# A mixer-and-experts layer on one core: expert biases split on 128 partitions, the largest expert moved within the order of experts

## The chip, the cores and the metric

The kernel runs on one NeuronCore of a Trainium2 chip. The metric is device time in microseconds (us) of one execution; lower is better. TensorE is called PE below, VectorE DVE, ScalarE ACT, GpSimd POOL and SyncE SP.

## The reference

One layer over 512 tokens of width 1024: four head groups run side by side (stick-breaking attention, a gated linear recurrence, HGRN2, Mamba-2) from one input projection, then an output projection with a residual, then a mixture of 32 experts, of which each token takes 4, and a last RMSNorm. Cut to the part that the change touches:

```python
logits = (xt @ router_w + router_b).astype(jnp.float32)
top_logits, top_idx = lax.top_k(logits, TOP_K)
gates = jax.nn.softmax(top_logits, axis=-1)
def run_block(args):              # rows of one expert e
    tok, e = args
    hmid = xt[tok] @ w_gu[e] + b_gu[e]
    glu = jnp.minimum(hmid[:, 0::2], SWIGLU_LIMIT)
    lin = jnp.clip(hmid[:, 1::2], -SWIGLU_LIMIT, SWIGLU_LIMIT)
    act = glu * jax.nn.sigmoid(SWIGLU_ALPHA * glu) * (lin + 1.0)
    return act @ w_down[e] + b_down[e]
```

The weights of one expert are w_gu (1024 x 2048) and w_down (1024 x 1024) in float32: 12 MiB. All 32 experts are read, 384 MiB.

## The kernel before

**The mixer part** (tile_kernel) comes first. Its order is written out by hand: strings such as ORD1 and ORD2, in which each letter calls one step of one generator. In ORD1 the letters d are steps of the Mamba-2 loop (d_loop: VectorE multiplies decay blocks by score blocks at L1874, PE uses them at L1880, the output is scaled at L1885 and L1886), s are steps of the HGRN2 state (c_state), b is the normalisation of the recurrence (L1465 to L1472), and the seven letters m are the steps of moe_biases. After ORD1 come the products with w_out (L1823), whose weights ACT and DVE split in two (L1817, L1818), interleaved by ORD2 with the last normalisations; then ORD3, in which the router runs and the weights of the experts start to stream in.

**moe_biases** (L120 to L151) turns the two bias tables of 32 x 2048 and 32 x 1024 into parts that a matrix product can add up exactly: each bias of w_gu into three bfloat16 parts that lie on partitions 0-31, 32-63 and 64-95 of the tile bgu, each bias of w_down into a float32r part, the same again, and the rest, in the tile bd. It loads each half of a table three times, one copy per group of 32 partitions (L130), and then rounds (ACT) and subtracts (DVE) in place, on 96 or on 32 partitions by 1024 columns. Its ACT steps are L138, L141, L142, L145 (twice each) and L149, its DVE steps L139, L143 (twice each) and L150.

**The experts** (moe) run in the order of the string SEQ. H stands for a large expert (up to 128 rows, more than 64), L for one with 64 rows, B for one with 32. The number of rows is a fixed capacity by the rank of the expert's count (CAPS); the H of the string with number BIG, counted from 0, is the largest expert: 128 rows as an H unit and 32 more as a B unit beside it. So before, the largest expert is the third H, expert number 7 of the order (counted from 0).

- An H unit uses three float32r products per weight block: the rows and the weights are both split into a high and a low part. ACT (L613) and DVE (L614) split each block of 128 x 1024 weights just before PE uses it (three(), L629), with three split buffers (NSP).
- An L or B unit feeds float32 weights straight to PE (L658 for w_gu, L729 and L724 for w_down).
- For expert j of the order, PE does the bias product (L644) and w_gu of j (gemm1), then the activation is started (act), then PE does w_down of expert j-1 (gemm2). When j-1 is an H, the outputs of the units before it are added to the rows of the tokens by products with one-hot matrices S (add, L789 on PE and L791 on DVE), interleaved with gemm2; with the largest expert they all stand before gemm2.
- yout scales and splits the output of a unit (ACT L742 and L761, DVE L744 and L763). For the largest expert it does the B unit first, whose output lies on 32 partitions at a time, four ACT and four DVE instructions.
- The rows of an expert are fetched by an indirect DMA on POOL (fetch, L568) and turned by PE (turn, L585). turn_at calls the turns of the groups that a table (where) puts at that place. That table follows from SEQ: the rows of an H form a group of their own, those of L and B units are put together, up to 128. Before, the group of experts 8 and 10 is turned right after the largest expert's gemm1 (place M at j = 7). prepare() makes one-hot matrices and fetches rows ahead.

**The weights** are read by SP in pieces of 1 MiB, 8 for w_gu and 4 for w_down, in the order in which PE uses them (Loads). They go round 11 places (pools ring and more; two further places at the beginning). A piece is read once the piece 11 before it has been used: by the split of an H, by the products of an L. SP takes its queue strictly in order; in front of the weights it has the loads of x into acc (L1958).

**The first expert** (j = 0) runs its gemm1 beside the rest of the router's tables, a generator called first, of nine steps: one step after each of the eight w_gu pieces, and, by the argument of mid, one more in the middle of pieces 4 to 7.

**The end**: gemm2 of the last expert is interleaved with add of the expert before it; hot builds the one-hot matrices S (L770) for both just ahead.

Of the kernel before, what the change touches and what calls it, by code (L numbers as in the profile page):

```python
# [21 lines left out]
F32 = mybir.dt.float32  # L22
FR = mybir.dt.float32r
BF = mybir.dt.bfloat16
I32 = mybir.dt.int32
U32 = mybir.dt.uint32
AF = mybir.ActivationFunctionType
OP = mybir.AluOpType
# [23 lines left out]

CAPS = (160, 120, 104, 104, 96, 96, 88, 80, 80, 72, 72, 72, 72) + 16 * (64,) + (32, 64, 64)

SEQ, BIG = "LL" + 4 * "HLHLL" + 3 * "HL" + "HBHL", 2
NSP = 3
FIN = "aaqqrAQrASQrAQrSSss"

# [59 lines left out]

def moe_biases(tc, a, bp, st, r_):

    nc = tc.nc
    bgu = bp.tile([96, 2048], BF, name="bgu")
    bd = bp.tile([96, D], FR, tag="yS", name="bd")
    r_["b"] = bgu, bd
    bst = [st[0:96, 0:1024], st[0:96, 1024:2048]]

    def load(f):
        src = a["moe_b_down"][0] if f == 2 else a["moe_b_gu"][0, :, 1024 * f:1024 * f + 1024]
        for s in range(3):
            nc.gpsimd.dma_start(bst[f % 2][32 * s:32 * s + 32, :], src)  # L130

    load(0)
    load(1)
    yield
    for f in range(2):
        cols = slice(1024 * f, 1024 * f + 1024)
        b = bst[f]
        nc.scalar.activation(bgu[:, cols], b, AF.Copy)  # L138
        nc.vector.tensor_tensor(b, b, bgu[:, cols], op=OP.subtract)  # L139
        yield  # L140
        nc.scalar.activation(bgu[32:64, cols], b[32:64, :], AF.Copy)  # L141
        nc.scalar.activation(bgu[64:96, cols], b[64:96, :], AF.Copy)  # L142
        nc.vector.tensor_tensor(b[64:96, :], b[64:96, :], bgu[64:96, cols], op=OP.subtract)  # L143
        yield
        nc.scalar.activation(bgu[64:96, cols], b[64:96, :], AF.Copy)  # L145
        if f == 0:
            load(2)
    yield
    nc.scalar.activation(bd, bst[0], AF.Copy)  # L149
    nc.vector.tensor_tensor(bd[64:96, :], bst[0][64:96, :], bd[64:96, :].bitcast(F32), op=OP.subtract)  # L150
    yield  # L151


# [325 lines left out]
def moe(ctx, tc, a, out, acc, c, loads, rt, mp, mp_es, hp, s2p, bp, early, once_es):  # L479

    nc = tc.nc
# [4 lines left out]
    def bank():  # L486
        return ps["m"].tile([128, 512], F32, name="m")

    def pair():

        return hp.tile([128, 1024], F32, name="h")
# [19 lines left out]
    cols = {x: [r for r, n in enumerate(CAPS) if n in ns] for x, ns in (("H", range(65, 129)), ("L", (64,)), ("B", (32,)))}  # L511
# [8 lines left out]
    N = len(seq)  # L520
# [125 lines left out]
    def gemm1(us, chunk, k, splits, limit, mid=lambda: None):  # L646

        W = chunk(k)
        last = k == KD - 1
        for u in us:  # L650
            if u.kind == "H":
                for half in range(2):
                    wh, wl = splits.take()
                    three(u.h[2 * half:2 * half + 2], u.xH[:, k, :], u.xL[:, k, :], wh, wl, False, last)
                    splits.make(limit)
            else:
                for q in range(4):
                    nc.tensor.matmul(u.h[q], u.xT[:, k, :], W[:, 512 * q:512 * q + 512], start=False, stop=last)  # L658
                    if q == 1:
                        mid()  # L660
# [104 lines left out]
    def hot(us):  # L765

        for u in us:
            if u.S is None:
                u.S = wk.tile([128, T], FR, name="S", bufs=3)[0:u.m]
                nc.vector.tensor_scalar(u.S, iota[0:u.m, :], u.tok[0:u.m, :], None, op0=OP.is_equal)  # L770
# [22 lines left out]
    splits = Splits([loads.of(j) for j, us in enumerate(seq) if us[0].kind == "H"])  # L793
# [3 lines left out]
    for g, us in enumerate(groups):  # L797
        j = us[0][0].j
# [21 lines left out]
    def turn_at(x, j, banks):  # L820
        for g in where.get((x, j), []):
            while g not in have:
                prepare()
            turn(g, *have[g], banks())
            turned.add(g)

    two = lambda: [bank(), bank()]
    halves2 = lambda: (lambda h: [h[:, 0:512], h[:, 512:1024]])(pair())

    def steps(*gens):  # L830
        for g in gens:
            yield from g

    def run(g, n=1000):
        for _ in range(n):
            if next(g, "end") == "end":
                return
# [5 lines left out]
    first = steps(rt.tables(), rt.more())  # L843
# [6 lines left out]
            ids(seq[e][0])  # L850
            yield

    pending = []
    for j, us in enumerate(seq):
        u = us[0]
        kind = u.kind
        if j == 1:
            once_es.close()
            sp = splits.pool = ctx.enter_context(tc.tile_pool(name="sp", bufs=NSP))
        if j == 2:  # L860
            mp_es.close()
            hL = ctx.enter_context(tc.tile_pool(name="hL", bufs=1, space=PSUM, side="right"))
            ps["m"] = ctx.enter_context(tc.tile_pool(name="m2", bufs=2, space=PSUM, side="right"))
        if j >= 1:
            loads.before(j + 1)

        if j == 0:
            u.views, u.h = [(0, rt.h0[0])], rt.h0[1]
        else:
            hL_ = [pair() if j < 2 else hL.tile([128, 1024], F32, name="hL")] if us[-1].kind != "H" else None  # L870
            light = lambda: hL_
            for x in us:
                if x.kind == "H":
                    x.bk = [pair(), pair()]
                bias(x, x.bk if x.kind == "H" else light() if x.kind == "L" else [light()[0][:, 0:512]])
        hi = heavy.index(j) if kind == "H" else 0
        after = heavy.index(j - 1) if j and seq[j - 1][0].kind == "H" else None
        for k in range(KD):
            if j == 0:
                gemm1(us, loads.of(j), k, splits, (hi, 16), lambda: run(first, k > 3))  # L880
                run(first, 1)
                continue
            gemm1(us, loads.of(j), k, splits, (hi, 16))
            if j == 1:
                if k == 0:
                    run(first)
                elif k < 5:
                    prepare()
                if k == 3:
                    back(seq[0])  # L890
                if k == 5:
                    mine = own()
                if k > 4:
                    run(mine, 2 if k == 7 else 1)
            elif k % 2:
                prepare()
            if kind == "H" and k == 2:
                turn_at("A", j, two)
            if kind != "H" and j > 1:
                if k == 3:  # L900
                    hot(pending)
                if after is not None and k > 4:
                    splits.make((after, 24), 1)
        act(us)
        if j == 0:
            continue
        if j > 1:
            turn_at("M", j, halves2 if kind != "H" and j > 1 else (lambda: [hL_[0][:, 512:1024], bank()]) if len(us) > 1 else two)

        prev = seq[j - 1]  # L910
        pk = prev[0].kind
        if pk == "H":
            hot(pending)
            limit = (after, 24) if kind != "H" and not (j + 1 < N and seq[j + 1][0].kind == "H") else (after + 1, 16)
            if len(prev) > 1:
                for i in range(NT):
                    add(pending, i)
        else:
            limit = None
        if j == 1:  # L920
            bd = rt.bdown()
        for f in range(KD):
            if pk == "H" and len(prev) == 1 and pending and 0 < f <= NT:
                add(pending, f - 1)
            gemm2(prev, loads.of(j - 1), f, splits, limit, u.views[0][1][:, 512:1024] if len(prev) > 1 else None)
            if j == 1:
                run(bd, 1)
                if f == 2:
                    turn_at("M", j, two)
                if f == 5:  # L930
                    back(us)
            elif pk != "H" and f in (2, 5):
                prepare()
            if pk == "H" and f == 4 and kind != "H":
                back(us)
            if f == 6 and len(us) > 1:
                back(us[1:])
            if pk == "H" and f == 5:
                turn_at("B", j, halves2)
            if pk != "H" and j + 1 < N and seq[j + 1][0].kind == "H" and f > 4:  # L940
                splits.make((heavy.index(j + 1), 16), 1)
        if pk == "H":
            pending = []
        pending = pending + prev
        yout(prev)
        if j > 1 and (pk != "H" or kind == "H"):
            back(us[:1])

# [62 lines left out]
    with tc.If(nblk > 0):  # L1011
        with tc.For_i(0, nblk, 1) as b, tc.manual_schedule():
# [11 lines left out]
            def chunk(q):  # L1024
                if q not in got:
                    got[q] = moe_chunk(nc, loads.slots, a, reg, q)
                return got[q]
# [999 lines left out]
```

## Time and profile before

| | us |
|---|---|
| median of 3 runs | 1378.11 |
| lowest and highest run | 1372.44, 1380.81 |
| the profiled execution, its own time | 1376.71 |
| its span, first to last instruction | 1374.9 |
| PE busy in the span | 1312.0 (95%) |
| DVE busy | 882.4 (64%) |
| ACT busy | 643.6 (47%) |
| read from HBM | 436.68 MB |

The profiled execution lies 1.4 us below the median, and 1.8 us of it are outside the span. The mixer part fills the span up to about 330 us, the experts follow, the last norm takes the end from about 1355 us. In rows of the trace an instruction is given as line, engine, operation, out<-in, shapes and count; what stands in square brackets is the idle time of that engine just before it and what ended it.

### The profile page before, as it was taken

The numbers are of one execution on the slowest core, as the hardware profiler recorded it, in microseconds if no ns is written. First come the engines' busy times: TensorE is split into PE (matmuls) and PEld (weight loads), VectorE is DVE, ScalarE is ACT, GpSimd is POOL, SyncE is SP. The second block draws the span as 40 slices with busy tenths as digits, with TensorE's granted clock in tenths as the row PEclk, the third lists the DMA queues.
The fourth block names the chain that finished last, engine by engine and source line by source line (L and its number), as shares of the span: only waits on it lengthen the run. The fifth ranks groups of instructions, "written<-read, shape, count | busy, mean of one in ns | idle before, by whom it ended". The sixth has DMA issues, their size and how long they took to land.

```text
span 1374.9 us, 17788 instructions
## 1 busy us (share of the span) xinstructions
PE 1312.0 (95%) x6460; PEld 768.3 (56%) x6460; DVE 882.4 (64%) x1215; ACT 643.6 (47%) x886; POOL 94.4 (7%) x162
## 2 busy tenths in 40 slices
PE   7999998898999999999999999999999999999994
PEld 6877773574365554456545655546544555464651
DVE  5457867675576754457546765748545667686865
ACT  5366667652154533336234542526334445454632
POOL 0000123020110002000010000200010000000001
PEclk9999997899999999999999999999999999999998
DMA  6312012087899999888999999999999999999982
GB/s 196 116 61 92 1 70 88 1 325 306 338 398 405 420 419 397 339 363 310 404 366 419 419 394 420 409 419 405 419 400 419 419 393 420 418 417 399 419 359 78
DMA packets 80801, 442.09 MB, mean 322 GB/s; under 512 B 10972, under 2 KB 25380, under 8 KB 31684
## 3 DMA queue, kind: packets, MB, share of 16 engines
q1 hardware_dynamic: 76708, 427.66, 77.7%
q0 software_dynamic: 3856, 12.72, 2.7%
q8 instruction: 52, 0.85, 0.3%
q10 hardware_dynamic: 144, 0.52, 0.1%
q14 instruction: 41, 0.34, 0.1%
HBM read 436.68 MB, written 4.19 MB: 321 GB/s over the span
## 4 chain that ended last, share of the span: by engine, by line
PE 77%; DMA 7%; DVE 7%; ACT 5%; issue 3%; POOL 1%; DVEq 0%; SPq 0%; ACTq 0%; POOLq 0%
PE h L629 18%; PE hL L658 14%; PE m L629 10%; PE m L729 7%; PE m L1198 6%; PE h L789 6%; DMA wch<-in_moe_w_down_dram 4%; DMA wch<-in_moe_w_gu_dram 3%; PE h L658 2%; DVE w L614 1%; PE h L1823 1%; PE m L1823 1%; PE h L696 1%; PE m L1202 1%; PE h L585 1%
## 5 line engine op out<-in xcount | busy, mean ns | idle before, releaser
L614 DVE TENSOR_TENSOR w<-wch,w 128x1024 fp32r<-128x1024 f32 x312 | 378.8, 1224 | 153.8 <-ACT w L613 145.5
L613 ACT ACTIVATE w<-wch 128x1024 fp32r<-128x1024 f32 x312 | 328.4, 1061 | 273.4 <-DMA wch<-in_moe_w_down_dram 98.7
L629 PE MATMUL h<-w,xx 128*72 128x512 f32 (+6 forms) x1248 | 301.9, 399 | 4.9 <-DVE w L614 4.5
L629 PEld LDWEIGHTS h<-w,xx 128*72 128x72 f32 (+6 forms) x1248 | 195.6, 159 | 102.8 <-DVE w L614 7.2
L658 PE MATMUL hL<-wch,xp 128*64 128x512 f32 (+1 forms) x1152 | 239.1, 593 | 1.1 <-DMA wch<-in_moe_w_gu_dram 1.1
L658 PEld LDWEIGHTS hL<-wch,xp 128*64 128x64 f32 (+1 forms) x1152 | 74.8, 134 | 148.8 <-issue 141.2
L729 PE MATMUL m<-wch,aTL 128*64 128x512 f32 x544 | 124.3, 603 | 0.2 <-DVE tg L557 0.2
L629 PE MATMUL m<-w,aH 128*72 128x512 f32 (+6 forms) x416 | 116.5, 400 | 3.4 <-ACT w L613 2.1
L675 ACT ACTIVATE ag<-ag 128x512 f32<-128x512 f32 (+7 forms) x46 | 28.6, 622 | 167.9 <-DVE ag L674 167.8
L629 PEld LDWEIGHTS m<-w,aH 128*72 128x72 f32 (+6 forms) x416 | 62.9, 158 | 39.7 <-issue 7.4
L565 POOL CAST ix<-tg 64x1 int32<-64x1 f32 (+8 forms) x31 | 19.0, 611 | 848.3 <-DVE tg L557 839.7
L791 DVE TENSOR_TENSOR acc<-acc,h 128x1024 f32<-128x1024 f32 (+1 forms) x61 | 72.9, 1198 | 6.4 <-PE h L789 6.4
L729 PEld LDWEIGHTS m<-wch,aTL 128*64 128x64 f32 x544 | 37.0, 138 | 69.2 <-issue 67.2
L763 DVE SCALAR_TENSOR_TENSOR yS<-m,tg,yS 64x512 fp32r<-64x512 f32 (+1 forms) x38 | 28.5, 750 | 71.4 <-ACT yS L761 71.0
L1198 PE MATMUL m<-uH,wh 128*128 128x512 f32 x176 | 71.9, 408 | 0.8 <-DVE uL L1305 0.8
L1198 PE MATMUL m<-uH,wl 128*128 128x512 f32 x176 | 70.1, 398 | 0.5 <-DVE wl L1164 0.4
L1198 PE MATMUL m<-uL,wh 128*128 128x512 f32 x176 | 69.9, 397 | 0.0
L629 PE MATMUL m<-w,aL 128*72 128x512 f32 (+6 forms) x208 | 65.1, 394 | 0.0
L761 ACT ACTIVATE yS<-m,tg 64x512 fp32r<-64x512 f32 (+1 forms) x38 | 25.9, 681 | 74.9 <-PE m L729 72.4
L789 PE MATMUL h<-yS,S 128*128 128x512 f32 (+1 forms) x168 | 54.9, 400 | 2.4 <-DVE acc L791 1.3
L674 DVE TENSOR_SCALAR ag<-hL 128x512 f32<-128x512 f32 (+1 forms) x18 | 11.9, 659 | 64.5 <-PE hL L658 64.5
L1164 DVE TENSOR_TENSOR wl<-wnat,wh 128x1024 fp32r<-128x1024 f32 (+1 forms) x26 | 31.5, 1223 | 30.3 <-ACT wh L1163 30.3
(500 smaller groups left out, 1634.0 us busy)
## 6 DMA issues: line engine op xcount, KB each, us to landing
wch<-in_moe_w_gu_dram SPq DMA_DIRECT2D x256, 1024.0 KB
wch<-in_moe_w_down_dram SPq DMA_DIRECT2D x127, 1024.0 KB
wnat<-in_w_in_dram SPq DMA_DIRECT2D x12, 1024.0 KB
wch<-in_w_out_dram SPq DMA_DIRECT2D x4, 1024.0 KB
xin<-in_x_dram SPq DMA_DIRECT2D x4, 512.0 KB
acc<-in_x_dram SPq DMA_DIRECT2D x4, 512.0 KB
xdr<-wch POOLq DMA_DIRECT2D x4, 512.0 KB, 7.5
out_dram<-fo SPq DMA_DIRECT2D x3, 512.0 KB
```

The costliest lines, as they stand in the source:

```text
L613: nc.scalar.activation(wh, w, AF.Copy)
L614: nc.vector.tensor_tensor(wl, w, wh.bitcast(F32), op=OP.subtract)
L629: nc.tensor.matmul(ps_[q], x, w[:, 512 * q:512 * q + 512], start=start and z == 0, stop=stop and z == 2)
L658: nc.tensor.matmul(u.h[q], u.xT[:, k, :], W[:, 512 * q:512 * q + 512], start=False, stop=last)
L675: nc.scalar.activation(g, g, AF.Gelu_apprx_sigmoid)
L729: nc.tensor.matmul(u.y[0][64 * dh:64 * dh + 64, :], u.aT[:, 2 * (f // 4) + f % 2, (f // 2) % 2, :], W[:, 512 * dh:512 * dh + 512], start=f ...
L763: nc.vector.scalar_tensor_tensor(u.yS[o_, dh, :], y[s_, :], u.gate[s_, :], u.yS[s_, dh, :].bitcast(F32), op0=OP.mult, op1=OP.subtract)
L789: nc.tensor.matmul(hh[:, 512 * dh:512 * dh + 512], s, y, start=z == 0, stop=z == len(todo) - 1)
L791: nc.vector.tensor_tensor(o, o, hh[:, cols], op=OP.add)
L1164: nc.vector.tensor_tensor(wl, w, wh.bitcast(F32), op=OP.subtract)
L1198: nc.tensor.matmul(s.p, s.ws[q // 2][:, k, :], u_[:, k, :], start=(k == 0 and q == 0), stop=(k == KD - 1 and q == 2))
L1823: nc.tensor.matmul(p, m_(x, k)[:, 128 * i:128 * i + 128], ww, start=(k == 0 and q == 0), stop=(k == KD - 1 and q == 2))
```

## The change

The bias tables are loaded once, on 128 partitions: a quarter of the columns on each group of 32 partitions, so that a step on 128 partitions has 512 (or 256) columns. The parts are made in a scratch tile and moved to their place in bgu and bd by 24 copies, 12 issued by SP and 12 by POOL. In the order of experts the second pair of L experts moves from places 20 and 21 to 26 and 27, and the largest expert becomes the fifth H, number 12 of the order. The extra B unit's output is evicted after two pieces of the next expert's gemm1 (late) and not ahead of them; turn_at for place M of the largest expert moves into gemm2 of the expert before; the first expert's extra router steps come in pieces 6 and 7 only; S for the last two units is built in the loop.

By the table where, the new order puts the 32 extra rows of the largest expert (12) into one group with the rows of expert 13, and this group and that of the largest expert's 128 rows are both turned at place M of j = 11. No group falls on place M of j = 12.

```diff
-SEQ, BIG = "LL" + 4 * "HLHLL" + 3 * "HL" + "HBHL", 2
+SEQ, BIG = "LL" + 3 * "HLHLL" + 4 * "HL" + "HLLHBHL", 4
...
-    bst = [st[0:96, 0:1024], st[0:96, 1024:2048]]
-
-    def load(f):
-        src = a["moe_b_down"][0] if f == 2 else a["moe_b_gu"][0, :, 1024 * f:1024 * f + 1024]
-        for s in range(3):
-            nc.gpsimd.dma_start(bst[f % 2][32 * s:32 * s + 32, :], src)
-
-    load(0)
-    load(1)
+    g, d = st[:, 0:512], st[:, 512:768]
+    parts = st[:, 768:1536].bitcast(BF).rearrange("p (s f) -> p s f", s=3)
+    dH, dL = st[:, 1536:1792].bitcast(FR), st[:, 1792:2048].bitcast(FR)
+    for q in range(4):
+        nc.gpsimd.dma_start(g[32 * q:32 * q + 32, :], a["moe_b_gu"][0, :, 512 * q:512 * q + 512])
+        nc.gpsimd.dma_start(d[32 * q:32 * q + 32, :], a["moe_b_down"][0, :, 256 * q:256 * q + 256])
     yield
-    for f in range(2):
-        cols = slice(1024 * f, 1024 * f + 1024)
-        b = bst[f]
-        nc.scalar.activation(bgu[:, cols], b, AF.Copy)
-        nc.vector.tensor_tensor(b, b, bgu[:, cols], op=OP.subtract)
-        yield
-        nc.scalar.activation(bgu[32:64, cols], b[32:64, :], AF.Copy)
-        nc.scalar.activation(bgu[64:96, cols], b[64:96, :], AF.Copy)
-        nc.vector.tensor_tensor(b[64:96, :], b[64:96, :], bgu[64:96, cols], op=OP.subtract)
-        yield
-        nc.scalar.activation(bgu[64:96, cols], b[64:96, :], AF.Copy)
-        if f == 0:
-            load(2)
+    nc.scalar.activation(parts[:, 0, :], g, AF.Copy)
+    nc.scalar.activation(dH, d, AF.Copy)
+    nc.vector.tensor_tensor(g, g, parts[:, 0, :], op=OP.subtract)
+    nc.vector.tensor_tensor(dL, d, dH.bitcast(F32), op=OP.subtract)
     yield
-    nc.scalar.activation(bd, bst[0], AF.Copy)
-    nc.vector.tensor_tensor(bd[64:96, :], bst[0][64:96, :], bd[64:96, :].bitcast(F32), op=OP.subtract)
+    nc.scalar.activation(parts[:, 1, :], g, AF.Copy)
+    nc.vector.tensor_tensor(g, g, parts[:, 1, :], op=OP.subtract)
+    yield
+    nc.scalar.activation(parts[:, 2, :], g, AF.Copy)
+    for s in range(3):
+        for q in range(4):
+            nc.sync.dma_start(bgu[32 * s:32 * s + 32, 512 * q:512 * q + 512], parts[32 * q:32 * q + 32, s, :])
+    for s in range(3):
+        for q in range(4):
+            nc.gpsimd.dma_start(bd[32 * s:32 * s + 32, 256 * q:256 * q + 256], (dH if s < 2 else dL)[32 * q:32 * q + 32, :])
     yield
...
             if j == 0:
-                gemm1(us, loads.of(j), k, splits, (hi, 16), lambda: run(first, k > 3))
+                gemm1(us, loads.of(j), k, splits, (hi, 16), lambda: run(first, k > 5))
...
             gemm1(us, loads.of(j), k, splits, (hi, 16))
+            if k == 1 and late:
+                yout(late)
+                late = []
...
-        if j > 1:
-            turn_at("M", j, halves2 if kind != "H" and j > 1 else (lambda: [hL_[0][:, 512:1024], bank()]) if len(us) > 1 else two)
+        if j > 1 and len(us) == 1:
+            turn_at("M", j, halves2 if kind != "H" else two)
...
+            if f == 4 and len(us) > 1:
+                turn_at("M", j, lambda: [hL_[0][:, 512:1024], bank()])
             if f == 6 and len(us) > 1:
                 back(us[1:])
+            if f == 6 and j == N - 1:
+                hot(prev + us)
...
-        yout(prev)
+        yout(prev[:1])
+        late = prev[1:]
```

## Rows read from the trace of the kernel before

**Rows 1.** The page: PE's busy time and instructions; the chain by engine.

```profile
PE 1312.0 (95%) x6460; PEld 768.3 (56%) x6460; DVE 882.4 (64%) x1215; ACT 643.6 (47%) x886; POOL 94.4 (7%) x162
...
PE 77%; DMA 7%; DVE 7%; ACT 5%; issue 3%; POOL 1%; DVEq 0%; SPq 0%; ACTq 0%; POOLq 0%
```

**Rows 2.** Windows: busy us of PE, PEld, DVE, ACT, POOL; PE clock, DMA share, GB/s.

```profile
530.00:660.00 130.00, 123.66 (x590) 68.94 (x588) 76.98 (x86) 55.27 (x65) 7.92 (x7) 0.96 0.89 345
660.00:1330.00 670.00, 664.82 (x3184) 358.76 (x3180) 438.61 (x499) 302.12 (x352) 27.28 (x31) 1.00 1.01 410
...
570.00:575.00 5.00, 4.09 (x16) 1.92 (x18) 1.97 (x5) 1.01 (x2) 0.00 (x0) 0.66 0.42 174
...
630.00:640.00 10.00, 9.41 (x32) 6.72 (x33) 6.61 (x8) 4.25 (x4) 1.18 (x2) 0.68 0.78 265
...
910.00:920.00 10.00, 9.01 (x42) 3.29 (x39) 2.49 (x3) 3.07 (x3) 0.00 (x0) 1.00 1.01 421
1060.00:1080.00 20.00, 16.62 (x74) 6.71 (x71) 5.70 (x7) 4.51 (x5) 0.00 (x0) 1.00 1.01 420
```

**Rows 3.** Chain that ended last, in order of time, 231 to 252 us: start, us, what.

```profile
231.61 1.21 DVE wch L139
...
247.92 1.22 DVE bd L150
...
251.14 0.79 PE m L1823
```

**Rows 4.** Timeline, 229 to 252 us: prices at 256 and 512 columns, PE's waits.

```profile
229.53 0.69 DVE L1886 TENSOR_TENSOR y<-y,zg 128x512 f32<-128x512 f32 x1
229.77 0.38 ACT L1901 ACTIVATE kn<-p 128x256 f32<-128x256 f32 x1 [2.69 <-PE p L1899]
236.87 2.00 PE L1880 MATMUL m<-wch,xd 128*64 128x384 f32 x4 [2.22 <-DVE wch L1874]
245.11 0.88 PE L1880 MATMUL m<-wch,xd 128*64 128x128 f32 x4 [2.79 <-DVE wch L1874]
```

**Rows 5.** Line 130, the loads of the biases: time from issue to landing.

```profile
DMA to landing us min/median/max: 2.4/2.9/3.0
```

**Rows 6.** Waits of SP's queue: us in total, times, longest.

```profile
SPq L1958 <- PE m L1823: 75.6, 1, 75.6
```

**Rows 7.** Timeline of PE after the largest expert's gemm1.

```profile
570.91 0.66 PE L585 MATMUL hL<-ident,rows 128*128 128x128 f32 x4 [2.85 <-DVE avB L677]
...
572.19 4.17 PE L729 MATMUL m<-wch,aTL 128*64 128x512 f32 x12
```

**Rows 8.** Timeline after the largest expert's gemm2, with the split of the weights.

```profile
622.13 2.76 ACT L761 ACTIVATE yS<-hL,tg 32x512 fp32r<-32x512 f32 x4
...
624.93 3.03 DVE L763 SCALAR_TENSOR_TENSOR yS<-hL,tg,yS 32x512 fp32r<-32x512 f32 x4 [1.50 <-ACT yS L761]
...
630.59 2.04 PE L629 MATMUL h<-w,xx 128*104 128x512 f32 x4 [2.68 <-DVE w L614]
...
636.72 1.23 DVE L614 TENSOR_TENSOR w<-wch,w 128x1024 fp32r<-128x1024 f32 x1 [1.68 <-ACT w L613]
```

**Rows 9.** The whole chain: starts of gemm1 of experts 7, 12, 14, 17; expert 28's weights.

```profile
536.11 3.00 PE h L629 x12
...
718.50 21.99 PE h L629 x96
...
783.70 5.49 PE h L629 x24
...
871.27 8.29 PE h L629 x36
...
1251.00 9.97 DMA wch<-in_moe_w_down_dram
```

**Rows 10.** Timeline: PE's wait in the first expert, and at the last adds.

```profile
342.08 0.32 PE L419 MATMUL m<-sc,early 32*96 32x1 f32 x2 [0.96 <-DVE sc L417]
...
1343.31 0.47 PE L789 MATMUL h<-yH,S 72*128 72x512 f32 x1 [1.45 <-DVE S L770]
```

More of the change, by code (lines that the diff above doesn't have):

```diff
@@ L851, in own @@
             yield
-    pending = []
+    pending, late = [], []
     for j, us in enumerate(seq):
```

## The prediction

> **What bounds the kernel now.** I read the page first, then windows of the whole span, then the chain that ended last, and at last the timeline at the places that the change touches. The page has PE busy for 1312.0 of 1374.9 us and 77% of the chain on PE [rows 1]: what shortens the kernel is work or waiting taken from PE's own line, and no more than 63 us of that line are idle. The windows add the second bound. From 660 to 1330 us PE is busy for 664.8 of 670 us, and in the same stretch the weights stream at 410 GB/s, where 420 is what they reach when PE stands and waits for them [rows 2]. So both run at their limit, coupled by the 11 places for weight pieces. One expert is 12 MiB, 12.58 MB, which at 410 GB/s (the fetches of rows included) is 30.7 us of stream. An H with an L behind it takes PE 65.2 us (718.50 to 783.70) and the stream 61.4; an H with two Ls takes PE 87.6 (783.70 to 871.27) and the stream 92.1 [rows 9]. A pair HL therefore gains the stream a lead of 3.8 us, a triple HLL costs it 4.5. When the lead is gone, PE waits: 1.0 us at 910 to 920 and 3.4 at 1060 to 1080 [rows 2], 4.4 in all. When the lead fills the 11 places, the stream waits: from 530 to 660 us, around the largest expert, it runs at 345 GB/s, which is 23 us of stream lost [rows 2]. The mixer part is another matter: there PE waits for ACT and DVE, which hand the biases back and forth on the chain [rows 3].
>
> **The biases.** Of the chain between 231.61 and 249.1 us, ten pieces from moe_biases, first and last in [rows 3], make up about 11.4 us (five ACT steps of 1.06, five DVE steps of 1.21 to 1.23). Nine ACT and five DVE steps leave. What comes: on ACT three steps on 512 columns and one on 256, on DVE two on 512 and one on 256. By the nearest rows of these sizes, 0.69 us for DVE at 512 and 0.38 for ACT at 256 [rows 4], and about 0.6 for ACT at 512 (between 0.38 at 256 and 1.06 at 1024), that is 2.2 us of ACT for 9.5 and 1.8 of DVE for 6.1. The gain is not the 11.4, for the rest of this stretch has a chain of its own. I went through it in program order. The DVE step at 235.0 can start 1.3 us earlier and is half as long, so that the next decay products start at 234.4 and not 236.25, and PE's wait of 2.22 us shrinks: 1.85 us. The three steps of the next m (7 us on the two engines) leave but for one ACT step, so the wait of 2.79 us goes too: PE reaches the last decay product at 240.3 and not 245.1. The bd step of 1.22 leaves just ahead of the last normalisation, so the first product with w_out starts at 245.1 and not 251.14 [rows 3, 4]: **6.0 us**. At least it should be the two waits less what replaces them, 3; at most 9, if that denser stretch also brings PE back to its full clock sooner. After that place the order is unchanged, and the load of x ahead of the weights in SP's queue waits for a product of PE until 276.65 [rows 6], so the stream starts 6 us earlier too.
>
> What comes in: 8 loads for 9, issued by POOL, and 24 copies. SP's 12 stand in its queue behind an ACT step at about 235 us; the next thing in that queue waits until 276 [rows 6], so they have 40 us. POOL's 12 wait for DVE's dL, done by then; POOL's next work is the router's constants after 277. A transfer of this kind takes 2.4 to 3.0 us to land [rows 5]; even one after the other, 12 take 36 us, and the biases are used only from 330 us. So their cost is nothing as long as the 40 us cover them; without the cover a late copy would delay the loads of x and the router by as much as it is late. The first rounding waits for the last load of the eight, 0.3 us, which is inside the 3 to 9.
>
> **The largest expert, its rows.** Before, the turn at 570.91 waits 2.85 us for DVE, PE then takes 1.3 us for eight turns at half clock, and the clock is 0.66 over 570 to 575, that is 3.4 us at 1.2 GHz, 1.7 lost [rows 2, 7]. With the new order no group falls on this place: its rows are turned at place M of j = 11, together with those of the H unit, ahead of an L's gemm2, beside which ACT and DVE can make the evictions. The turn itself costs PE the same 1.0 there. Saved: 2.85 and most of the half clock, **4.0 us**; bounds 1 (a second turn that waits for the eviction of the first) and 4.6.
>
> **The largest expert, its extra output.** Before, ACT needs 2.76 us and DVE 3.03 for the four small pieces, in front of the H output and of the next splits; PE runs out of split weights and waits 2.68 us, then has 6.4 us at half clock (0.68 over 630 to 640), 3.2 lost [rows 2, 8]: 5.9. After, the same pieces come after four of sixteen half pieces of the next gemm1. There DVE takes 1.23 us per split [rows 8] and PE 21.99/16 = 1.37 per half piece [rows 9], so DVE has only 0.14 us to spare in each. Behind the late ACT and DVE instructions wait the next splits, and PE waits for those: 3.03 less what three ready buffers leave free, I take 2.0 us of stall, in two pieces. Saved: **4.0 us**. Bounds: 5.9 if the buffers hide it; 0.5 if the stall is the whole 3.0 and the clock falls again. The trace has all three: a wait of 2.68 us and one of 2.85 were each followed by half clock, and a loss of 3.4 us in several pieces at 1060 to 1080 was not (1.00) [rows 2, 7, 8]. The Trainium skill (TensorE: Matmul & The Clock Gate, section HAM oscillation) holds that waits between bursts of products put the engine back to half clock at each such place anew. By that rule the late eviction costs 2.0 + 3.2 and saves 0.7, and the sum below is 3.3 us smaller; by the row at 1060 it does not.
>
> **The first expert and the end.** The wait of 0.96 us at 342.08 [rows 10] stands between two router steps that are now a whole weight piece apart: 0.8 saved; bounds 0 (DVE's last tables end later and the activation behind them with it) and 1.3. At the end PE waits 1.45 us until the second matrix S [rows 10]; with S built before, what is late next is DVE's yL, which stands right ahead of S in DVE's queue: I take 0.5, bounds 0 and 1.4.
>
> **The lead of the stream.** The waits of 4.4 us at 910 and 1060 come after two groups HLHLL in a row behind the largest expert. After the change its surplus comes at j = 12, followed by HLL and four HL, so these waits go. But the triple HLL now stands just ahead of the B expert, where before an HL stood and the weights came just in time (a piece of 9.97 us of the chain at 1251 is w_down) [rows 9]. There the lead is 4.5 + 3.8 = 8.3 us lower; the HL pairs ahead of it give back up to 2 x 3.8 = 7.6 if the places are not full already. So new waits of 0.7 to 8.3 us; 3.0, nearer to the low end, since the first pairs behind the largest expert find the places full but the later ones do not. Net gain **1.4 us**, bounds -3.9 and 3.7.
>
> **Sum.** 6.0 + 4.0 + 4.0 + 0.8 + 0.5 + 1.4 = 16.7 us. The profiled execution took 1376.7, so 1360.0; it lay 1.4 below the median of the runs, so on their scale 1361.4. I give 1361. With all low ends 9.0 + 4.6 + 5.9 + 1.3 + 1.4 + 3.7 = 25.9, with all high ends 3 + 1 + 0.5 + 0 + 0 - 3.9 = 0.6; the forecast's own range is 1353 to 1368.
>
> **Rivals.**
> The stream sets the end. The 410 GB/s without a pause from 660 to 1330 speak for it; against it speaks that the whole trace has only 4.4 us of plain waits for it. Then what the largest expert gives back is waited off later; only the earlier start of the stream counts: 6.0 us, 1372 on the runs' scale.
>
> The stream sets the end and loses more: slower. It decides itself in the four HL pairs in a row. If the places are full when they begin, each pair leaves the stream idle for up to 65.2 - 2 x 30.0 (an expert at 420 GB/s) = 5.2 us, 20.8 in all, that the last triple and the B expert must wait for at the end, while the loss at the largest expert stays at 23. Then 1378 - 6 + 20.8 = 1393. It needs an idle stream of over 20 us between the largest expert and j = 25; the two HL pairs at the end of the order before show no such loss, as the mean of 410 up to 1330 says [rows 2].
>
> The bias part saves little: another chain (PE at half clock, the normalisations) binds in 231 to 251 us, and 1 of 6 is left: 1366. For it speaks that four of the chain's pieces there are not of the biases; against it the ten that are.
>
> The change does not do what it says at the largest expert: the late eviction stalls PE for 3 us and the clock halves, the two turns in one place cost as much as the one did: 8 less, 1369.
>
> **How the numbers follow.** Forecast 0.57; stream sets the end 0.18; slower by the stream 0.04; biases save little 0.12; nothing at the largest expert 0.09. The range, 1352 to 1372, holds the forecast's own range, the two partial failures and half of the first rival. What a measurement of this kernel can tell from no change is about 1%, 13.8 us: faster means under 1364.3. The forecast gives 0.52 of that, the rest of the cases 0.08: faster 0.6. The slower case ends at 1.1%, half of it beyond the bound: slower 0.03, the rest 0.37.
>
> **What would show it.** In the profile after: the first product with w_out some 6 us earlier, and the load of x at about 271 instead of 276.65; no idle PE and no half clock after the largest expert's gemm1; a wait under 2.5 us in the gemm1 of j = 14 with the clock at 1.00; no wait for weights between j = 13 and j = 25; a few us of it around the B expert. It is wrong if the last weights land as late as before (the stream then sets the end), if the stretch 229 to 251 is as long as before, or if the stream runs below 400 GB/s through the four HL pairs.

## The result, and the profile after

The changed kernel takes 1359.18 us (median of 4 runs, 1358.75 to 1360.46), the kernel before 1377.42 (4 runs) beside it: ratio 0.9874, interval 0.9847 to 0.9901. The profiled execution of after took 1360.46 us with a span of 1358.6, so between the two profiled executions 16.3 us are gone. The time forecast (1361) is right; the terms behind it are not all right, as the sections below show.

Lines of the experts' part have moved up by 3 (L629 is L626 now, L658 is L655, L613 and L614 are L610 and L611, L761 and L763 are L758 and L760), those of the mixer down by 5.

The page of after, PE's busy time and the chain by engine, against [rows 1]:

```profile
PE 1306.8 (96%) x6460; PEld 767.4 (56%) x6460; DVE 878.1 (65%) x1213; ACT 637.1 (47%) x881; POOL 102.2 (8%) x173
...
PE 84%; DVE 6%; ACT 5%; issue 2%; DMA 1%; POOL 1%; DVEq 0%; ACTq 0%; POOLq 0%
```

PE has as many instructions as before and is busy 5.2 us less, since less of its work runs at **half clock** (a granted clock of 0.50, 1.2 GHz; 3.4 us of it lose 1.7 us of work); the other 11 us were waits. The chain now has 84% on PE for 77%, and 1% on DMA for 7%.

Windows of after (busy us of PE, PEld, DVE, ACT, POOL; PE clock, DMA share, GB/s), against [rows 2]; the first two stretches are the same ones:

```profile
530.00:660.00 130.00, 129.83 (x611) 74.92 (x611) 86.03 (x96) 57.82 (x66) 3.59 (x5) 1.00 1.01 419
660.00:1330.00 670.00, 661.76 (x3179) 355.67 (x3174) 435.03 (x494) 300.28 (x350) 31.55 (x31) 0.99 0.98 394
...
770.00:780.00 10.00, 6.96 (x26) 4.98 (x26) 8.10 (x10) 5.59 (x7) 2.99 (x2) 0.83 0.61 237
1060.00:1080.00 20.00, 20.00 (x91) 10.13 (x89) 13.73 (x15) 9.02 (x10) 0.61 (x1) 1.00 1.00 406
1230.00:1240.00 10.00, 9.00 (x76) 3.02 (x72) 3.11 (x6) 2.08 (x4) 0.00 (x0) 1.00 1.01 420
1240.00:1250.00 10.00, 6.76 (x22) 4.00 (x23) 5.43 (x7) 4.44 (x5) 0.00 (x0) 0.71 1.01 419
```

From 530 to 660 us PE no longer waits; the largest expert is now at 680 to 761. The 3.4 us of waits at 1060 are gone. Two places are new: 3.0 idle us at 770 to 780 and 4.2 at 1230 to 1250, each with a clock under 1.00.

The first of them, in the timeline of ACT, DVE and PE in gemm1 of j = 14, against [rows 8]:

```profile
767.65 2.74 ACT L758 ACTIVATE yS<-hL,tg 32x512 fp32r<-32x512 f32 x4
...
770.42 2.00 ACT L610 ACTIVATE w<-wch 128x1024 fp32r<-128x1024 f32 x2
770.43 3.03 DVE L760 SCALAR_TENSOR_TENSOR yS<-hL,tg,yS 32x512 fp32r<-32x512 f32 x4 [1.42 <-ACT yS L758]
772.45 0.60 ACT L590 ACTIVATE xp<-m 128x512 f32<-128x512 f32 x1
...
773.10 1.05 PE L582 MATMUL m<-ident,rows 128*128 128x128 f32 x4 [3.04 <-ACT xp L590]
```

The late pieces are the rows of 2.74 and 3.03 us. By the releaser, PE waits 3.04 us at a turn whose first half's eviction (L590) stands in ACT's queue behind the late pieces and two splits. Then 3.4 us run at half clock (0.83 over 10 us is 1.7 lost).

The second, in the timelines of PE and ACT at the B expert (unit B of expert 29, right behind HLL and the H of expert 28), with one step of the chain there:

```profile
1240.12 1.07 PE L655 MATMUL hL<-wch,xp 128*32 128x512 f32 x8 [1.12 <-DMA wch<-in_moe_w_gu_dram]
1243.77 0.72 PE L626 MATMUL m<-w,aH 128*72 128x512 f32 x2 [2.58 <-ACT w L610]
```
```profile
1242.66 2.02 ACT L610 ACTIVATE w<-wch 128x1024 fp32r<-128x1024 f32 x2 [8.94 <-DMA wch<-in_moe_w_down_dram]
```
```profile
1228.16 14.41 DMA wch<-in_moe_w_down_dram
```

ACT ends the wait of 2.58 us, but ACT itself had stood idle 8.94 us for that w_down: the weights set it.

The chain in the stretch of the biases, against [rows 3]:

```profile
233.75 0.60 DVE wch L139
...
239.35 0.76 DVE y L1890
...
243.92 2.34 PE m L1828 x5
```

Of moe_biases one DVE step of 0.60 us (and 0.10 of its queue) is left on the chain. PE's waits of 2.22 and 2.79 us [rows 4] are gone, the longest left is one of 1.31 us for a step of the HGRN2 state (L1930), and the first product with w_out starts at 243.11 and not 251.14.

### The profile page after: what moved, and what is told of

Same layout as the page of the kernel before. It is cut to its first block, busy times and chain, and to the rows that moved or that the text cites. A ratio compares the mean times of both kernels' runs of the same rounds, so it can differ in the third digit from the quotient of the medians.

```text
span 1358.6 us, 17829 instructions
## 1 busy us (share of the span) xinstructions
PE 1306.8 (96%) x6460; PEld 767.4 (56%) x6460; DVE 878.1 (65%) x1213; ACT 637.1 (47%) x881; POOL 102.2 (8%) x173
## 4 chain that ended last, share of the span: by engine, by line
PE 84%; DVE 6%; ACT 5%; issue 2%; DMA 1%; POOL 1%; DVEq 0%; ACTq 0%; POOLq 0%
PE h L626 19%; PE hL L655 17%; PE m L626 11%; PE m L726 9%; PE m L1203 7%; PE h L786 6%; PE h L655 2%; DVE w L611 1%; PE h L1828 1%; PE h L693 1%; DMA wch<-in_moe_w_down_dram 1%; PE m L1828 1%; PE m L1207 1%; ACT w L610 1%; PE h L641 1%
## 5 line engine op out<-in xcount | busy, mean ns | idle before, releaser
L611 DVE TENSOR_TENSOR w<-wch,w 128x1024 fp32r<-128x1024 f32 x312 | 378.9, 1224 | 134.9 <-ACT w L610 127.0
L610 ACT ACTIVATE w<-wch 128x1024 fp32r<-128x1024 f32 x312 | 328.8, 1062 | 256.6 <-PE m L626 104.0
L626 PE MATMUL h<-w,xx 128*72 128x512 f32 (+6 forms) x1248 | 301.7, 398 | 2.4 <-DVE w L611 1.9
L626 PEld LDWEIGHTS h<-w,xx 128*72 128x72 f32 (+6 forms) x1248 | 194.6, 158 | 99.0 <-issue 6.0
L655 PE MATMUL hL<-wch,xp 128*64 128x512 f32 (+1 forms) x1152 | 238.4, 593 | 1.1 <-DMA wch<-in_moe_w_gu_dram 1.1
L655 PEld LDWEIGHTS hL<-wch,xp 128*64 128x64 f32 (+1 forms) x1152 | 75.0, 134 | 149.6 <-issue 143.2
L626 PE MATMUL m<-w,aH 128*72 128x512 f32 (+6 forms) x416 | 117.0, 402 | 3.1 <-ACT w L610 2.6
L626 PEld LDWEIGHTS m<-w,aH 128*72 128x72 f32 (+6 forms) x416 | 63.5, 159 | 39.7 <-issue 9.4
L760 DVE SCALAR_TENSOR_TENSOR yS<-m,tg,yS 64x512 fp32r<-64x512 f32 (+1 forms) x38 | 28.5, 750 | 74.3 <-ACT yS L758 74.0
L626 PE MATMUL m<-w,aL 128*72 128x512 f32 (+6 forms) x208 | 65.5, 396 | 0.0
L758 ACT ACTIVATE yS<-m,tg 64x512 fp32r<-64x512 f32 (+1 forms) x38 | 25.9, 682 | 78.3 <-PE m L726 75.8
```

The lines of the kernel that those rows point to most:

```text
L610: nc.scalar.activation(wh, w, AF.Copy)
L611: nc.vector.tensor_tensor(wl, w, wh.bitcast(F32), op=OP.subtract)
L626: nc.tensor.matmul(ps_[q], x, w[:, 512 * q:512 * q + 512], start=start and z == 0, stop=stop and z == 2)
L760: nc.vector.scalar_tensor_tensor(u.yS[o_, dh, :], y[s_, :], u.gate[s_, :], u.yS[s_, dh, :].bitcast(F32), op0=OP.mult, op1=OP.subtract)
```

## Experiments

Times are compared in two ways. A ratio is to the kernel before, run beside it. **The experts' part** is the time from the first expert's first product to the end of the last gemm2 in the profiled execution: 1024.5 us before, 1017.7 after. It leaves out the start, whose length changes between executions (last section); only in e6, e7, e9, e10 and e11 does the end of the start's half clock reach into it, 1.6 to 1.8 us that lose 0.8 to 0.9.

**The biases alone (e1).** The kernel before with the new moe_biases, nothing else.

```diff
-def moe_biases(tc, a, bp, st, r_):  # of before
+def moe_biases(tc, a, bp, st, r_):  # of after
```

> The kernel before with the new bias function alone. Forecast's step: first product with w_out 6.0 us earlier (at 245.1) and the whole 6.0 us shorter. Theory now, from the trace after (first product at 243.1, first load of a weight piece 8.9 us earlier): 8 to 9 us shorter than before, so 0.9935 to 0.994 of it; the stretch back at half clock after 244 lasts 3.5 us and not 13. Rival (biases save little, the rest of the start comes from elsewhere in the change): 0 to 2 us.

Measured: 0.9923 (0.9892 to 0.9954), medians 1364.85 and 1377.07. The first w_out product starts at 241.6, the first expert at 319.7 for 330.0; half clock after 243.0 for 3.4 us. The experts' part is 1022.9. So the biases give 10.6 us by the ratio (6.3 to 14.9): the 8 to 9 of the theory lie inside that interval, the 6.0 forecast just below it. In the profile 10.2 us are at the start; 1.6 are in the experts' part, most of it a shorter half clock behind the largest expert (3.4 us where before had 6.8). The waits of 2.85 and 2.69 us at the largest expert stay as in [rows 7, 8].

**The late pieces elsewhere (e2).**

```diff
-            if k == 1 and late:
-                yout(late)
-                late = []
...
             gemm2(prev, loads.of(j - 1), f, splits, limit, ...)
+            if f == 2 and late:
+                yout(late)
+                late = []
```

> The kernel after, with the largest expert's late four pieces of ACT and DVE moved from the heavy expert's gemm1 (j = 14, k = 1) into the light gemm2 that follows (f = 2), where no splits and no turn stand behind them. Theory: the wait of 3.04 us at 770.06 and the half clock after it (1.7 us) go, gemm1 of j = 14 takes about 24.3 us and not 29.0, and the whole is 4 to 4.7 us shorter than after, 0.9966 of it. Rival A (the stream sets the end from here): PE comes 4.7 us earlier to the B expert and waits that much longer there, 0 us. Rival B (the pieces are too long for the 7 us of the light gemm2): a new wait of 2 to 3 us where the next gemm begins, gain 1 to 2 us.

Measured: 0.9826 (0.9781 to 0.9871), 1352.22 us; experts' part 1010.1, 7.6 less than after. gemm1 of j = 14 takes 24.1 us and not 29.0, 4.9 of the gain. ACT and DVE do the same 2.74 and 3.03 us beside the light gemm2, and PE waits for nothing there, so rival B falls:

```profile
786.74 7.09 PE L726 MATMUL m<-wch,aTL 128*64 128x512 f32 x32
788.11 2.74 ACT L758 ACTIVATE yS<-hL,tg 32x512 fp32r<-32x512 f32 x4
790.88 3.03 DVE L760 SCALAR_TENSOR_TENSOR yS<-hL,tg,yS 32x512 fp32r<-32x512 f32 x4 [0.95 <-ACT yS L758]
```

Rival A falls too: the 4.9 us are not waited off later, for at the B expert the wait of 2.58 us has not grown. The rest of the gain is there, but does not follow from the edit: half clock lasted 3.4 us and not 6.8, and the first wait, of 1.12 us in after, was shorter (gemm1 7.4 us for 8.4).

**The triple one pair earlier (e3).**

```diff
-SEQ, BIG = "LL" + 3 * "HLHLL" + 4 * "HL" + "HLLHBHL", 4
+SEQ, BIG = "LL" + 3 * "HLHLL" + 3 * "HL" + "HLLHLHBHL", 4
```

> The kernel after, with the last triple HLL one pair earlier (after the largest expert: HLL, three HL, HLL, HL, HB, HL in place of HLL, four HL... the triple directly ahead of HB); nothing else. Theory: the waits for weights at the B expert (PE idle 1.1 and 2.6 us at 1240, half clock 1244 to 1251, 7 to 8 us in all) come from the triple and HB standing one behind the other; with a pair between, 3 to 4 us of them remain at most, so 3.5 to 7 us shorter than after. Rival (the stream has lost its time at the largest expert, and wherever the triple stands it is waited off once before the end): within 1.5 us of after.

Measured: 0.9843 (0.9796 to 0.9889), 1354.94 us; experts' part 1013.1, 4.6 less than after. At the B expert PE waits 0.5 us where it waited 3.7, its clock stays at 1.00, and no wait over 0.6 us appears anywhere from 775 to 1320 us:

```profile
1234.54 7.04 PE L655 MATMUL hL<-wch,xp 128*32 128x512 f32 x64
1242.06 0.69 PE L626 MATMUL m<-w,aH 128*72 128x512 f32 x2 [0.48 <-ACT w L610]
```

That is 3.2 us of waits and 3.4 lost to half clock, so about 2 of these 6.6 us were lost again in small pieces elsewhere. The rival falls: what is lost at the B expert hangs on the triple standing directly ahead of HB.

**The extra output at once (e4).**

```diff
-            if k == 1 and late:
-                yout(late)
-                late = []
...
-        yout(prev[:1])
-        late = prev[1:]
+        yout(prev)
```

> The kernel after, with the largest expert's extra output evicted together with its large output, as before the change; nothing else. The forecast's step (the late eviction saves 4.0 us): 4 us longer than after. Theory now (the late eviction stalls PE for 3.0 us and brings the half clock, as the one at once did with 2.7): within 1.5 us of after, with the wait and the half clock back in front of gemm1 of j = 14.

Measured: 0.9866 (0.982 to 0.9912), 1356.07 us. gemm1 of j = 14 takes 28.9 us, with a wait of 2.69 and half clock for 3.4 us: the eviction at once costs what the late one costs (29.0). So the forecast's 4.0 for this step falls. PE's waits there and at the B expert:

```profile
767.28 1.17 PE L626 MATMUL h<-w,xx 128*96 128x512 f32 x4 [2.69 <-DVE w L611]
...
1240.82 0.68 PE L626 MATMUL m<-w,aH 128*72 128x512 f32 x2 [2.43 <-ACT w L610]
```

The experts' part is 4.4 us shorter than after, nearly all of it at the B expert (4.2): the wait of 2.43 us was not followed by half clock this time, and the wait of 1.12 us ahead of it was not there.

**The order of before in the kernel after (e5).**

```diff
-SEQ, BIG = "LL" + 3 * "HLHLL" + 4 * "HL" + "HLLHBHL", 4
+SEQ, BIG = "LL" + 4 * "HLHLL" + 3 * "HL" + "HBHL", 2
```

> The kernel after with the order of before (largest expert third of the large ones); biases, late eviction, first expert and end stay as after. It prices the order. The forecast's steps for the order (4.0 for the rows, 1.4 for the stream, and the late eviction as in after): 5 us longer than after. Theory now: the order saves the 2.85 us and half clock after the largest expert's gemm1 less 2.6 us of turns moved ahead of it, and the 4.4 us of waits behind it, but costs 7.4 us at the B expert, so about 0; on top, the late eviction has no turn behind it in this order (no group is turned at k = 2 of j = 9), so its stall of 3.0 us should shrink to under 1.5: 0 to 4 us shorter than after. Rival (the stall is that of the splits, turn or not): the stall of about 3 us and a half clock stay at j = 9.

Measured: 0.9887 (0.9853 to 0.9922), 1360.98 us; experts' part 1019.6. Two things follow. First, in the timeline of PE behind the largest expert's gemm1 the turn now stands inside the light gemm2 and waits for nothing, where [rows 7] has 2.85 us:

```profile
555.40 4.51 PE L726 MATMUL m<-wch,aTL 128*64 128x512 f32 x20
559.85 0.65 PE L582 MATMUL hL<-ident,rows 128*128 128x128 f32 x4
560.34 0.60 PE L582 MATMUL m<-ident,rows 128*128 128x128 f32 x4
```

From the start of the largest expert's gemm1 to the next light gemm1 it is 43.2 us (523.4 to 566.6) for 47.6 before: 4.4 saved by the turn's new place in gemm2, with the old order. Second, the late pieces, with no turn behind them in this order, still stop PE, now for splits:

```profile
619.91 4.36 PE L626 MATMUL h<-w,xx 128*104 128x512 f32 x11 [2.72 <-DVE w L611]
```

So the rival is right on the stall: 3 us of small pieces on ACT and on DVE beside a heavy gemm1 are a stall of about 3 us, with a turn behind them (after) or without. The whole came out between the two sums: 1.9 us longer than after in the experts' part, where the forecast's steps give 5 longer and the theory 0 to 4 shorter. The times do not decide it, since the intervals of the ratios of e5 and after overlap.

**The order alone (e11).** As e5, with the late pieces in the light gemm2 as in e2.

> The order of before with all else as after and the late pieces in the light gemm2 that follows. Against the run with the same pieces and the order after it prices the order alone. Forecast's steps for the order: 4.0 us for the rows (less what the turn's new place gives by itself) and 1.4 for the stream, so 1.4 to 5.4 us longer than the run with the late pieces moved. Theory now (the turn's place under gemm2 gives the 4 us in either order; the waits for weights behind the largest expert are traded for those at the B expert): within 2 us of it, with 2 to 6 us of waits and half clock between 900 and 1080 us in place of those at 1240.

Measured: 0.9831 (0.9811 to 0.9851), 1354.68 us; experts' part 1013.4 for 1010.1 in e2; 0.8 of these 3.3 us is the first expert at half clock. gemm1 behind the largest expert takes 22.6 us; the waits for weights behind it are back (1.71 us at 1056.6, with 3.4 us of half clock). That puts the order at 2.5 us, as the medians do (1354.68 and 1352.22), inside the forecast's 1.4 to 5.4 and near the theory's 2. But the two ratios differ by 0.0005 with intervals that overlap, so a worth of nothing is not excluded.

**First expert and end undone (e7).**

```diff
-                gemm1(us, loads.of(j), k, splits, (hi, 16), lambda: run(first, k > 5))
+                gemm1(us, loads.of(j), k, splits, (hi, 16), lambda: run(first, k > 3))
...
-            if f == 6 and j == N - 1:
-                hot(prev + us)
```

> The kernel after without two small edits: the first expert's router steps again from the fifth weight piece, and the second matrix S of the end built where it was. Forecast: 0.8 and 0.5, 1.3 us longer than after. Theory now (from the trace after: 1.0 at the first expert, 1.1 at the end): 2.1 us longer, with the waits of 0.96 and 1.45 us back. Rival (the first expert's 1.0 us is waited off later for the stream): 1.1 us longer.

Measured: 0.9907 (0.9875 to 0.9939), 1364.01 us; experts' part 1019.8, 2.1 more than after. Both waits are back (0.96 and 1.46 us). By place, the first expert takes 1.9 us more, 0.9 of it half clock from the start, so 1.0, and the last gemm2 13.7 us for 12.6, so 1.1: the theory's 2.1. That the sum is 2.1 as well is chance, for 1.5 us more at expert 8 and 2.5 less at the B expert stand in it too. The median is 4.8 above that of after; the rest is not put down to these edits, since in the profiled execution the start alone had half clock for 13.7 us where after had 3.4.

**Both mended (e6, e10), beside after again (e9).** The edits of e2 and e3 together; e10 is the same kernel as e6, on the chip of e9 and e11.

> The kernel after with both mended: the late pieces in the light gemm2 of j = 14 and the last triple one pair earlier. Theory (the two are apart and both are PE's waits): no wait at 770, one of at most 2.5 us for weights near the B expert, 4 to 5 us shorter than the run with the late pieces alone moved and the run with the triple alone moved, so 1347 to 1350 us. Rival (the stream sets the end once one of them is mended): 1352 to 1355, with the time given back as waits for weights between 1100 and 1300 us.

> The kernel after, unchanged, beside the next two on the same chip. Theory (in all runs with the new biases PE waits 1.3 us at 239 and the stretch to the first expert is the same; what differs is how long the half clock lasts after 311: 3.4, 10.2 or 13.7 us): 1357 to 1361 us, first expert's gemm1 between 318 and 325 us.

> The kernel with the late pieces in the light gemm2 and the triple one pair earlier, again, beside after. Theory: no wait for weights and none for ACT or DVE of over 1 us from the first expert to the end but the few that both have; 8 to 11 us shorter than after (3.0 + 1.7 us at 770, 1.1 + 2.6 us of waits and up to 3.4 lost to half clock at the B expert). Rival (half of that was the luck of the half clock after 311): 4 us.

Measured: e6 0.9806 (0.9779 to 0.9833), 1350.75 us; e10 0.982 (0.9798 to 0.9842), 1352.49 us; e9 0.9859 (0.9844 to 0.9874), 1357.52 us, inside the 1357 to 1361 expected. The experts' parts are 1009.3, 1008.5 and 1018.6. PE's longest waits in e6, from 330 to 1340 us (us in total, times, longest):

```profile
PE h L626 <- DVE w L611: 2.0, 6, 0.7
PE h L786 <- DVE acc L788: 1.2, 3, 0.5
PE m L626 <- DVE w L611: 1.1, 2, 0.6
```

No wait is over 0.8 us, and none ends on a DMA, as the theory has it. The gain is less clear. The experts' part of e10 is 10 us under that of e9, but 6.8 of this is half clock (7.6 us lost in e9, 0.9 in e10), and e9's profiled execution is the slowest of its five. By the medians beside each other the gain is 5.0 us, by the ratios of e10 and e6 against e9 5 to 7: below the theory's 8 to 11 and nearer to the rival's 4. e6 has the lowest median of the kernels run, 1350.75 where its theory had 1347 to 1350, but the ratios of e2, e8 and e11 lie within its interval. What the earlier triple adds to e2 is thus shown at its place in the profile and not by the times.

**The largest expert later (e8).** Late pieces as in e2.

```diff
-SEQ, BIG = "LL" + 3 * "HLHLL" + 4 * "HL" + "HLLHBHL", 4
+SEQ, BIG = "LLHLLHLHLHLHLLHLLHLHLLHLHLHLHBHL", 6
```

> An order in which the largest expert comes when the stream has no lead to lose: LL, HLL, three HL, two HLL, then HL with the largest expert (seventh of the large ones), HLL, three HL, HB, HL; late pieces in the next light gemm2, all else as after. Theory (the waits at the B expert are the stream lost while the places are full at the largest expert, 237 to 342 GB/s there in the kernel after): the stream keeps 400 GB/s or more through the largest expert and no wait for weights over 1 us is left anywhere: 2 to 4 us shorter than the kernel with both mended. Rival (the waits depend on the triple's distance to the B expert alone): as the kernel with both mended within 1.5 us.

Measured: 0.983 (0.9791 to 0.987), 1353.36 us; experts' part 1009.9. There is one wait for weights, 1.57 us at 504.7, behind the triple that now comes first. Through the largest expert the stream runs at 383 GB/s (836 to 918 us), against 380 in after (680 to 761) and 348 before (536 to 623). So the theory is wrong: the stream does not keep 400 GB/s there, one wait over 1 us is left, and the kernel is not 2 to 4 us shorter than e6 but 0.6 longer in the experts' part and 2.6 by the median. The rival (as e6 within 1.5 us) is not contradicted, since the intervals of the two ratios overlap.

## Why the prediction was right in sum

| Step of the forecast | Forecast (bounds) | Measured |
|---|---|---|
| the biases | 6.0 (3 to 9) | 8.8 at the first expert; alone 10.2 |
| largest expert's rows | 4.0 (1 to 4.6) | 5.1 |
| its extra output | 4.0 (0.5 to 5.9) | 1.0 in these two profiles; 0 by e4 |
| first expert | 0.8 (0 to 1.3) | 1.0 |
| end | 0.5 (0 to 1.4) | 1.1 |
| lead of the stream | 1.4 (-3.9 to 3.7) | -2.9 |
| sum | 16.7 | 14.1 of 16.3 |

**Biases: too small.** Windows from 225 us to the first w_out product, before and after (columns as above):

```profile
225.00:251.10 26.10, 18.57 (x151) 9.71 (x150) 16.06 (x27) 15.23 (x25) 3.73 (x8) 0.80 0.16 46
```
```profile
225.00:243.10 18.10, 15.58 (x151) 8.37 (x150) 11.36 (x25) 7.95 (x20) 9.10 (x19) 1.00 0.30 67
```

The stretch is 8.0 us shorter. PE's idle time falls from 7.5 to 2.5 us, 5.0, a little under the 6.0 worked out from the waits. The other 3.0 are the same 151 products at a clock of 1.00 for 0.80. The forecast named this as its upper bound and did not take it. The load of x starts at 267.6 for 276.65, where the forecast had 271, and the weights follow: 271.1 for 280.0. The copies cost nothing seen: SP's last is issued at 238.7, and SP's next load waits for PE in any case; POOL's take 1.8 us (median) to land.

**Largest expert's rows: right, and a little too small.** No group is turned at that place any more, and PE's wait of 2.85 us and the half clock behind it are gone, as forecast. The gain is 47.6 us before against 41.3 after (680.4 to 721.7) from the start of the largest expert's gemm1 to the next light gemm1, less 1.2, by which the two turns at M of j = 11 lengthen the step from gemm1 to the light gemm2 there (1.8 us for 0.6); the turn itself costs about what it did before, as the forecast took it. What the forecast left out: the change also moves the turn into the light gemm2 (f = 4), and e5 shows that this gives 4.4 us in the old order as well. In the kernel after, that edit has nothing to do; either of the two would have been enough for most of this step.

**Extra output: the step that failed.** The forecast took a stall of 2.0 us without half clock. The runs show 3.04 us and 3.4 us of half clock in after, 2.72 and 3.4 in e5, 2.69 and 3.4 when evicted at once in e4. The cost is gemm1's length less that without the pieces: before 28.5 - 22.6 (e11) = 5.9, as forecast; after 29.0 - 24.1 (e2) = 4.9. Even this 1.0 is luck: it is the half clock, which lasted 6.8 us in the profile before and 3.4 in after. In e1, with the order and the eviction of before, it lasted 3.4 and the cost is 27.4 - 22.6 = 4.8; in e9, which is after again, it lasted 6.8. The three ready buffers hid 0.3 us of the 3.03 at most. That fits DVE's 0.14 us to spare per half piece, which the forecast had and did not let decide; no run varies the number of buffers.

The Trainium skill (TensorE: Matmul & The Clock Gate, section HAM oscillation) tells of a kernel that fell back to half clock at every wait between its bursts of products; those waits were of about 3 to 5 us, where the forecast applied it to 2.0. At this place the runs agree: all eight profiled executions with the stall (waits of 2.68 to 3.04 us) have half clock behind it. Elsewhere they do not: the 2.43 us at the B expert in e4 and the 1.70 us at 1072 in the kernel before were followed by a clock of 1.00.

**Lead of the stream: the other step that failed, by size.** The waits of 4.4 us went as said. The new one was put at 3.0 of 0.7 to 8.3; it is 7.3: 1.4 in the B expert's gemm1 (8.4 us for 7.0), 2.6 ahead of the heavy gemm2, 3.3 in it (23.1 for the 19.8 that a heavy gemm2 behind a triple has elsewhere in after). Most of the 3.3 is half clock, which no term held and which the same place has for 0 to 6.8 us (last section). The place was right, and e3 shows the mechanism as forecast: a pair between the triple and HB takes it away.

**The rivals.** That the stream sets the end is out: what e2 takes from PE at j = 14 is not waited off later, and the four HL pairs (854 to 1113 us) run at 410 GB/s with PE busy for 258.9 of 259 us. "The change does not do what it says at the largest expert" was right in its half on the late eviction, wrong on the turns. That the biases save little is out by e1.

**The signs.** Of what the forecast named to look for, all came but one: the wait in gemm1 of j = 14 is 3.04 us at a clock of 0.83, not under 2.5 at 1.00.

That the sum came out is in part luck: two terms were 3.0 and 4.3 us too high and the others 4.7 too low, and about 2 us more were gained, in pieces under 1 us that are not traced to an edit.

## What to carry to other kernels

Here small evictions cost nothing only beside a stretch in which the engine that does them had time: compare its time per step with PE's there, and move them to a step where it has some. Price a wait of PE with the half clock that may follow it, and give the term both values. A sum can be right with two wrong terms; experiments that undo one part each show which.

## What was not expected of the hardware

The same wait does not always bring half clock, nor the same length of it. Between about 309 and 330 us all kernels with the new biases do the same work with waits under 0.9 us. The window in after, in e5 and in e9, which is after again (columns as above):

```profile
310.00:330.00 20.00, 17.49 (x90) 8.83 (x90) 8.27 (x33) 4.86 (x10) 0.72 (x3) 0.91 0.70 266
```
```profile
310.00:330.00 20.00, 18.14 (x99) 8.43 (x100) 9.56 (x40) 3.37 (x7) 0.72 (x3) 1.00 0.73 280
```
```profile
310.00:330.00 20.00, 17.74 (x70) 8.80 (x70) 7.43 (x27) 4.58 (x9) 0.72 (x3) 0.66 0.48 189
```

A clock of 0.91, 1.00 and 0.66 over 20 us is 3.6, 0 and 13.6 us at 1.2 GHz, so the first expert starts at 321.2, 318.4 and 324.1. In e9 the profiled execution took 1364.31 us at a mean clock of 0.975, the four others 1356.09 to 1357.72 at 0.980 to 0.982. The stall of 3.04 us at j = 14 was followed by 3.4 us of half clock in after, e3 and e7 and by 6.8 in e9. At the B expert a wait of 2.58 us was followed by 6.8 us of half clock in after and 3.4 in e2, one of 2.43 by none in e4; a wait of 1.7 us behind a triple by none before, 6.8 us in e5 and 3.4 in e11. What decides it these runs do not show. Differences of two profiled executions under 5 us are therefore read here by place, and not by their sums.
